# Modulations taken one at a time, a convolution's weights ahead of the first head's decay strips, and two norm broadcasts earlier in TensorE's order

## The chip, the core and the metric

The kernel runs on one core of a Trainium2 chip. The metric is the device time of one execution in microseconds (us), lower is better. A core has five engines that run at the same time, each through its own list of instructions in order: TensorE (PE, matmuls), VectorE (DVE), ScalarE (ACT), GpSimd (POOL) and SyncE (SP). Here SP and POOL mostly issue transfers (DMAs) from memory. An instruction at the head of its engine's list waits on semaphores for the work of other engines, and everything behind it on that engine waits with it.

## The reference

One layer of a diffusion backbone for 512 latent and 256 context tokens of 1024 channels. `c` is the conditioning vector; from it nine modulation vectors (shift, scale and gate, three times) come by one large product.

```python
mods = jnp.split((jax.nn.silu(c) @ w_mod[layer] + b_mod[layer])[:, None, :], N_MOD, axis=-1)
sh1, sc1, g1, sh2, sc2, g2, sh3, sc3, g3 = mods          # the context has its own, from c_ctx
h  = h + 0.5 * g1 * swiglu(modulate(h, norm_ffn1, sh1, sc1), w_ffn1_in, w_ffn1_out)
hc = hc + 0.5 * g1c * swiglu(modulate(hc, norm_ffn1, sh1c, sc1c), w_ffn1_in, w_ffn1_out)
u, uc = modulate(h, norm_mix, sh2, sc2), modulate(hc, norm_mix, sh2c, sc2c)
kv_c = uc @ w_in[:, K0:G0]                               # context keys and values: start states
q, k, v, rg, cv, ga, gb = jnp.split(u @ w_in, IN_SPLITS, axis=-1)
q, k = rope_2d(q, rows, cols), rope_2d(k, rows, cols) * qk_scale
o, _, _ = bidir_retention(q, k, v, log_gf, log_gb, rf, rb)   # 4 heads, decayed scores both ways
h = h + g2 * mixer_output(o, rg, cv, ga, gb, ...)        # gated with a 31-wide depthwise convolution
h = h + 0.5 * g3 * swiglu(modulate(h, norm_ffn2, sh3, sc3), w_ffn2_in, w_ffn2_out)
return rmsnorm(h, final_norm)
```

`modulate(x, w, sh, sc)` is `rmsnorm(x, w) * (1 + sc) + sh`.

## The kernel before

Tokens lie along the free dimension, channels along the 128 partitions. Each product is written as three matmuls (`mm3`, lines 111 to 113): weights and activations are split into a rounded high part and a low rest, and high x high, high x low and low x high are summed. So every weight tile of 128x1024 costs a transfer into one of four `wraw` buffers, a rounding copy on ACT (`wh`, line 102) and a subtraction on DVE (`wl`, line 104).

The order of instructions on each engine isn't the order in which they are written. A scheduler takes the written order as a priority and puts each instruction where its own cost estimates say that its inputs are ready. An edit that moves a call in the text therefore moves instructions only where the scheduler's result changes.

The layer's stages on the time line of the profiled execution, in us from the span's start:

- Up to about 105: the first norm, the first eight modulations (`start`, `first_mods`) and the first products.
- To about 590: the first SwiGLU (`ffn1`). Its hidden blocks come in six groups (`GROUPS1`, of 4, 4, 4, 3, 3 and 4 blocks). A block of the later groups is a `chunk`, seven products of 12 matmuls of 384 columns (`product`, line 404). Behind each group stands the output part: for `mm` in 0 to 3 a weight tile and the products of its two output blocks, added into memory by POOL (`part_sum`). The hidden blocks `hx` are split on ACT and DVE (`split`, lines 300 and 301) just before the output part needs them.
- The other 56 modulation pieces are spread over `ffn1`. `mod_step(count)` takes the next `count` of `MOD_STEPS`; each (`mods`) issues a 512 KB transfer on POOL's queue into one of two `wm` buffers (line 200), and DVE multiplies and sums it (line 206, once or twice). `STEPS_IN` and `STEPS_OUT` say how many fall in each group's chunks and in its output part; several are taken in one call.
- 590 to 650: the second norm and the first head. `tail1` and `head2` hang pieces of the norm between the products. The norm's factor is made per half of the tokens, 256 columns each (first half "a", second half "b"): `rstd_sum` sums squares with four small matmuls (lines 255 and 256), takes a square root on ACT (line 280) and a few small operations on DVE (lines 281 to 286), and makes a diagonal `dg` (line 262). `rstd_bcast` then spreads it over the partitions by one matmul with `ones` (line 269). `norm_mods` makes the normed halves `uh` and `ul` from it: line 291 on DVE, 292 on ACT, 293 on DVE, for each of eight channel blocks.
- In `retention(0)` the context's keys (`keys_c`, 48 matmuls of 256 columns) come first, then `rotated`: keys and queries, for each half of the tokens four products of 24 matmuls. DVE then rotates them (`roped`, lines 733 to 736, and the split in 301). `strips(0)` loads four tables of distances (lines 751 and 752), puts them through Exp on ACT (753, 754) and adds them on DVE (755); scores are multiplied by these strips later. `conv_chunk` (called by `conv_at`) makes one of eight convolution blocks: 48 matmuls of 512 columns and a long chain on DVE (line 716).
- 650 to 1200 the rest of the four heads, to 1380 gates and merging, then the second SwiGLU to the end.

Exp and Sqrt use different tables of ACT: a change from one to the other puts an `ACT_TABLE_LOAD` in its list.

## Time and profile before

| | |
|---|---|
| median of 3 runs | 1781.86 us (1779.5 to 1781.98) |
| the profiled execution's own time | 1779.1 us |
| its span, first to last instruction | 1777.0 us |
| mean granted TensorE clock | 0.985 |
| PE busy / idle in the span | 1723.9 us (97%) / 53.1 us |
| DVE, ACT, POOL busy | 1150.4, 676.0, 141.6 us |
| DMA | 221.97 MB, mean 125 GB/s |

The page and the views of the trace name each instruction by its line in the kernel, its engine, its operation and the tiles that it writes and reads. "Idle before, and what ended it" tells how long an engine sat still before an instruction and whose work released it. PEclk is the clock that TensorE was granted, 1.00 being full speed. Since PE is busy for 97% of the span, the time can fall only where PE waits or where its clock is lowered.

### The profile page before, as it was taken

The numbers are of one execution on the slowest core, as the hardware profiler recorded it, in microseconds if no ns is written. First come the engines' busy times: TensorE is split into PE (matmuls) and PEld (weight loads), VectorE is DVE, ScalarE is ACT, GpSimd is POOL, SyncE is SP. The second block draws the span as 40 slices with busy tenths as digits, with TensorE's granted clock in tenths as the row PEclk, the third lists the DMA queues.
The fourth block names the chain that finished last, engine by engine and source line by source line (L and its number), as shares of the span: only waits on it lengthen the run. The fifth ranks groups of instructions, "written<-read, shape, count | busy, mean of one in ns | idle before, by whom it ended". The sixth has DMA issues, their size and how long they took to land.

```text
span 1777.0 us, 22523 instructions
## 1 busy us (share of the span) xinstructions
PE 1723.9 (97%) x8930; PEld 1498.8 (84%) x8930; DVE 1150.4 (65%) x1818; ACT 676.0 (38%) x969; POOL 141.6 (8%) x221
## 2 busy tenths in 40 slices
PE   5999999999999889999999999999999999999997
PEld 3689999989899878888888888888788988888887
DVE  5895868786677788793885679293765643333335
ACT  4644434434344522342342334233563432222222
POOL 3401020202112100010000000001100000000000
PEclk7999999999999999999999999999999999999999
DMA  9347373857665321142142115115552133222221
GB/s 347 110 143 154 120 182 109 196 177 195 201 171 177 109 83 60 69 157 72 52 156 87 55 69 176 60 48 177 191 196 100 60 119 95 100 95 99 98 84 48
DMA packets 68254, 221.97 MB, mean 125 GB/s; under 512 B 8178, under 2 KB 9202, under 8 KB 68148
## 3 DMA queue, kind: packets, MB, share of 16 engines
q1 hardware_dynamic: 45652, 146.84, 24.6%
q0 software_dynamic: 21920, 72.64, 14.6%
q8 instruction: 70, 1.15, 0.3%
q10 hardware_dynamic: 576, 1.05, 0.2%
q14 instruction: 36, 0.29, 0.0%
HBM read 192.18 MB, written 31.46 MB: 126 GB/s over the span
## 4 chain that ended last, share of the span: by engine, by line
PE 80%; issue 6%; DMA 6%; DVE 6%; ACT 1%; POOL 1%; SPq 0%; DVEq 0%; POOLq 0%; ACTq 0%
PE ps L112 23%; PE ps L113 23%; PE ps L111 23%; PE ps L404 9%; DMA wm<-in_w_mod 2%; DMA th<-in_w_mod 2%; DVE wl L104 1%; DVE h L716 1%; DMA wraw<-in_w_co 1%; DMA wraw<-in_w_v 0%; DMA kl<-in_dec 0%; POOL hdram L620 0%; DVE t L206 0%; DVE t L183 0%; PE ps L895 0%
## 5 line engine op out<-in xcount | busy, mean ns | idle before, releaser
L102 ACT CAST wh<-wraw 128x1024 fp32r<-128x1024 f32 (+2 forms) x212 | 219.5, 1037 | 559.9 <-PE ps L112 309.2
L104 DVE TENSOR_TENSOR wl<-wraw,wh 128x1024 fp32r<-128x1024 f32 (+2 forms) x212 | 254.4, 1203 | 198.3 <-ACT wh L102 193.5
L111 PE MATMUL ps<-uh,wh 128*128 128x512 f32 (+1 forms) x924 | 332.3, 362 | 1.5 <-ACT uh L292 1.1
L113 PE MATMUL ps<-uh,wl 128*128 128x512 f32 (+1 forms) x924 | 331.0, 359 | 0.0
L112 PE MATMUL ps<-ul,wh 128*128 128x512 f32 (+1 forms) x832 | 298.5, 360 | 0.2
L112 PE MATMUL ps<-gx,wh 128*128 128x512 f32 (+1 forms) x544 | 204.0, 377 | 0.0
L113 PE MATMUL ps<-gx,wl 128*128 128x512 f32 (+1 forms) x544 | 204.0, 377 | 0.0
L111 PE MATMUL ps<-gx,wh 128*128 128x512 f32 (+1 forms) x544 | 203.7, 377 | 0.2 <-ACT gx L300 0.2
L111 PEld LDWEIGHTS ps<-uh,wh 128*128 128x128 f32 x924 | 174.8, 190 | 28.2 <-ACT uh L292 1.5
L113 PEld LDWEIGHTS ps<-uh,wl 128*128 128x128 f32 x924 | 175.7, 190 | 25.4 <-issue 0.2
L716 DVE SCALAR_TENSOR_TENSOR h<-y,vec,h 128x512 f32<-128x512 f32 x240 | 179.7, 749 | 5.5
L112 PEld LDWEIGHTS ps<-ul,wh 128*128 128x128 f32 x832 | 158.4, 191 | 24.4 <-issue 0.9
L111 PE MATMUL ps<-hx,wh 128*128 128x512 f32 (+1 forms) x368 | 122.0, 335 | 7.4 <-ACT hx L300 7.4
L112 PE MATMUL ps<-hx,wh 128*128 128x512 f32 (+1 forms) x368 | 123.1, 335 | 0.0
L113 PE MATMUL ps<-hx,wl 128*128 128x512 f32 (+1 forms) x368 | 122.7, 334 | 0.0
L111 PEld LDWEIGHTS ps<-gx,wh 128*128 128x128 f32 x544 | 102.1, 188 | 19.2 <-ACT gx L300 0.4
L112 PEld LDWEIGHTS ps<-gx,wh 128*128 128x128 f32 x544 | 102.0, 188 | 18.7
L113 PEld LDWEIGHTS ps<-gx,wl 128*128 128x128 f32 x544 | 102.0, 188 | 18.7
L359 DVE TENSOR_TENSOR wl<-wraw,wh 128x1024 fp32r<-128x1024 f32 x54 | 66.1, 1224 | 54.5 <-ACT wh L358 54.2
L404 PE MATMUL ps<-th,wl 128*128 128x384 f32 x288 | 96.2, 334 | 0.0
L404 PE MATMUL ps<-th,wh 128*128 128x384 f32 x288 | 96.2, 334 | 0.0
L404 PE MATMUL ps<-tl,wh 128*128 128x384 f32 x288 | 96.2, 334 | 0.0
(277 smaller groups left out, 3109.4 us busy)
## 6 DMA issues: line engine op xcount, KB each, us to landing
wm<-in_w_mod POOLq DMA_DIRECT2D x56, 512.0 KB, 4.5
wraw<-in_w1i SPq DMA_DIRECT2D x44, 512.0 KB, 6.5
wraw<-in_w2i SPq DMA_DIRECT2D x44, 512.0 KB, 3.6
hdram<-sg POOLq DMA_DIRECT2D x40, 384.0 KB, 7.5
wraw<-in_w1o SPq DMA_DIRECT2D x16, 512.0 KB, 3.5
wraw<-in_w_cv SPq DMA_DIRECT2D x16, 512.0 KB, 4.3
wraw<-in_w_v SPq DMA_DIRECT2D x16, 512.0 KB, 6.0
wraw<-in_w_rg SPq DMA_DIRECT2D x16, 512.0 KB, 3.6
```

The lines of the kernel that those rows point to most:

```text
L102: nc.scalar.copy(hi, raw)
L104: nc.vector.tensor_sub(lo, raw, f32(hi))
L111: nc.tensor.matmul(o, w[0], x[0], start=first, stop=False)
L112: nc.tensor.matmul(o, w[0], x[1], start=False, stop=False)
L113: nc.tensor.matmul(o, w[1], x[0], start=False, stop=last)
L359: nc.vector.tensor_sub(lo, src, f32(hi))
L404: nc.tensor.matmul(o, w[i][:, ws], x[k][m], start=first and k == n == 0, stop=k == 3 and n == 2, skip_group_check=True)
L716: nc.vector.scalar_tensor_tensor(o, y[:, t:t + L], vec[:, w0 + t:w0 + t + 1], o, ALU.mult, ALU.add)
```

## The change

Three edits. First, `mod_step` is no longer called with several pieces at a time at the end of a chunk or ahead of an output tile: `spread` deals `STEPS_IN` out over two places in each chunk (one between its products, one behind it, none behind the group's last) and `STEPS_OUT` over the eight output blocks. Second, in the first head `conv_at(0)` is called ahead of `strips(0)`. Third, the first half's broadcast moves from the end of `ffn1` into the context keys: `head2(0)` is called within the first product of `keys_c` and makes the broadcast and all eight blocks; and the second half's broadcast (`head2(2)`) is called behind the first of the four products of `rotated`, not behind the fourth.

```diff
-    def chunk(j, u, t, keep):
+    def chunk(j, u, t, beside, keep):
...
         nc.scalar.activation(s[:, lo_], pa, AF.Silu)
+        beside()
         product(pd, w1, 1, [x[3] for x in t], False)
...
+            steps = spread(STEPS_IN[gi], 2 * nk - 1)
+            beside = lambda: mod_step(next(steps))
             for j in range(2 if k0 == 0 else 0, nk):
...
                 elif k0:
-                    keep(j, chunk(k0 + j, u, t, None))
+                    keep(j, chunk(k0 + j, u, t, beside, None))
+                    beside()
                 if k0:
-                    mod_step(STEPS_IN[gi] * (j + 1) // nk - STEPS_IN[gi] * j // nk)
                     continue
...
+            steps = spread(STEPS_OUT[gi], 8)
             for mm in () if last else range(4):
-                mod_step(STEPS_OUT[gi] * (mm + 1) // 4 - STEPS_OUT[gi] * mm // 4)
...
                 for i in range(2):
+                    beside()
                     part_sum(2 * mm + i, px[i], pc[i][:, :LC])
...
+    def spread(total, slots):
+        return (total * (i + 1) // slots - total * i // slots for i in range(slots))
...
         if n == 4:
             st["a"] = rstd_sum(acc, st["sq", 0], HALVES[0])
-        if n == 6:
-            st["ra"] = rstd_bcast(st["a"])
-        if n == 7:
-            norm_mods(h, st["ra"], deriv["x2"], st["u"], HALVES[0], range(4))
...
         if n == 0:
+            ra = rstd_bcast(st["a"])
+            norm_mods(h, ra, deriv["x2"], u, HALVES[0], range(4))
             st["b"] = rstd_sum(acc, st["sq", 256], HALVES[1])
-            norm_mods(h, st["ra"], deriv["x2"], u, HALVES[0], range(4, KT))
+            norm_mods(h, ra, deriv["x2"], u, HALVES[0], range(4, KT))
...
-                proj(pc[:, i, :], wk[i], uc)
-                if hd == 0:
-                    head2(i)
+                for ks in (range(4), range(4, KT)):
+                    proj(pc[:, i, :], wk[i], uc, ks)
+                    if hd == i == ks[0] == 0:
+                        head2(0)
...
                     proj(px[i][:, c], w[i], u, c=c)
-                if hook:
-                    hook()
-                    hook = None
+                    if hook:
+                        hook()
+                        hook = None
...
+            conv_at(hd)
             sx, sc = strips(hd)
-            conv_at(hd)
```

What becomes of this in the engines' lists, at three places.

DVE at the end of the fourth group (390 us in the profile), where the last hidden block is split and four modulations stand between its steps. Line 206 is a modulation, 421 to 433 the last block's arithmetic, 301 its split. First the kernel before:

```order
L206 SCALAR_TENSOR_TENSOR t_3632,mx<-wm_3630,kh_84 128x1024
L419 TENSOR_TENSOR t_3461<-t_3461,ps_3458 128x384
L230 TENSOR_TENSOR g_x_3634<-mx,vec 128x8
L104 TENSOR_TENSOR wl_3702<-wraw_3698,wh_3700 128x768
L421 TENSOR_TENSOR sg_3464<-ps_3460,t_3461 128x384
```

and the changed one at the same place (its line 420 is 419 of before, 422 is 421):

```order
L206 SCALAR_TENSOR_TENSOR t_3678,mx<-wm_3676,kh_84 128x1024
L420 TENSOR_TENSOR t_3461<-t_3461,ps_3458 128x384
L230 TENSOR_TENSOR g_x_3680<-mx,vec 128x8
L104 TENSOR_TENSOR wl_3698<-wraw_3694,wh_3696 128x768
L422 TENSOR_TENSOR sg_3464<-ps_3460,t_3461 128x384
```

Nothing moved: only the buffers' numbers differ. From the fourth group on, the lists of DVE, ACT and POOL and the waits in them are the same in both kernels up to about 575 us. The first edit changes DVE's list around the first group's output part (some 40 rows), a few neighbours around the second and the third group's, and on POOL's queue the place of one `wm` transfer, which now stands behind two `hdram` sums and not ahead of them.

ACT at the start of the second norm (585 us in the profile). The first Sqrt (line 280) belongs to half "a", the casts (102) to the query weights, lines 292 to the normed blocks. Before:

```order
L102 CAST wh_5661<-wraw_5659 128x1024
L753 ACTIVATE sc_5938<-wraw_5946,lg 128x640
L245 ACTIVATE t_5447<-gx_926_5048 128x256
L280 ACT_TABLE_LOAD
L280 ACTIVATE t_5457<-ps_5451,epsb 128x2
L102 CAST wh_5667<-wraw_5665 128x1024
L754 ACT_TABLE_LOAD
L754 ACTIVATE wraw_5947<-wraw_5947,lg 128x640
```

Now, from that Sqrt to the second one, which belongs to half "b" (lines 758 and 759 are 753 and 754 of before, 783 is 777):

```order
L280 ACTIVATE t_5457<-ps_5451,epsb 128x2
L102 CAST wh_5667<-wraw_5665 128x1024
L245 ACTIVATE t_5480<-gx_927_5049 128x256
L245 ACTIVATE t_5497<-gx_928_5050 128x256
L292 ACTIVATE uh_970_5279<-t_5573,ab_x_3140 128x256
L292 ACTIVATE uh_972_5281<-t_5577,ab_x_3140 128x256
L758 ACT_TABLE_LOAD
L758 ACTIVATE sx_6037<-wraw_6039,lg 128x896
L292 ACTIVATE uh_974_5283<-t_5581,ab_x_3140 128x256
L292 ACTIVATE uh_976_5285<-t_5585,ab_x_3140 128x256
L280 ACT_TABLE_LOAD
L280 ACTIVATE t_5595<-ps_5589,epsb 128x2
```

The strips' Exps left the neighbourhood of half "a"'s Sqrt, which needs no table load any more. The first of them now stands between the normed blocks, ahead of half "b"'s Sqrt. On SP's queue the two transfers of the convolution's weights moved ahead of the strips' four.

PE around the two broadcasts (line 269). Before, the first stands behind the last product of `ffn1` (`hx`), and the second behind all 96 matmuls of the first half:

```order
L113 MATMUL ps_5358<-hx_897_4895,wl_5090 128x256
L269 MATMUL ps_5501<-t_5464,ones 128x256
L111 MATMUL ps_5576<-uh_970_5279,wh_5566 128x256
...
L113 MATMUL ps_5674<-uh_984_5293,wl_5669 128x256
L269 MATMUL ps_5771<-t_5614,ones 128x256
L111 MATMUL ps_5671<-uh_970_5279,wh_5566 128x256
```

Now the first has 27 of the 48 matmuls of the context's keys (`ps_5558`) ahead of it, and the second 12 of the first half's 96 (`ps_5671`):

```order
L113 MATMUL ps_5558<-uh_970_5279,wl_5556 128x256
L269 MATMUL ps_5571<-t_5464,ones 128x256
L111 MATMUL ps_5558<-uh_972_5281,wh_5554 128x256
...
L113 MATMUL ps_5671<-uh_976_5285,wl_5550 128x256
L269 MATMUL ps_5699<-t_5602,ones 128x256
L111 MATMUL ps_5672<-uh_970_5279,wh_5554 128x256
```

Between the two broadcasts PE has 9 matmuls of the context's keys, half "b"'s four small sums, 12 more of the keys and the 12 of the first half. Further on, the 48 matmuls of the convolution block now stand whole ahead of the first scores; before, 4 of them stood ahead and 44 behind the first 11 of the 36 scores' matmuls. DVE makes the low part of the convolution's second weight tile (line 104) behind most of the four rotations, as before.

## The prediction, made before the changed kernel ran

> **What bounds the kernel now.** I read the list of waits of PE first, since PE is busy for 97% of the span (the table above), then each wait in PE's timeline, then the granted clock in short windows, and last DVE and ACT ahead of each wait.

> ```profile
> PE ps L269 <- DVE t L262: 8.7, 3, 5.4
> PE ps L111 <- ACT hx L300: 7.4, 2, 3.8
> PE ps L111 <- ACT gx L300: 4.7, 2, 4.5
> PE ps L111 <- ACT uh L292: 1.1, 1, 1.1
> 594.68 0.79 PE L269 MATMUL ps<-t,ones 128*128 128x256 f32 x1 [5.43 <-DVE t L262]
> 616.91 0.74 PE L111 MATMUL ps<-uh,wh 128*128 128x256 f32 x4 [1.12 <-ACT uh L292]
> 634.26 0.80 PE L111 MATMUL ps<-gx,kh 128*128 128x256 f32 x2 [4.49 <-ACT gx L300]
> ```

> The reader is to see three waits within 45 us, 11.04 us together, all in the stretch that the second and third edit rewrite; and two of 7.4 us in `ffn1`, which the first edit names. Most of the rest of PE's 53 us idle lies at the start and the end of the kernel.

> A wait costs more than its length, since the clock falls. Windows behind the waits at 594.68 and 634.26 (columns: PE, PEld, DVE, ACT, POOL, PEclk, DMA):

> ```profile
> 595.00:597.00 2.00, 2.00 (x9) 1.82 (x9) 1.78 (x5) 0.55 (x2) 0.00 (x0) 0.50 0.90 277
> 597.00:599.00 2.00, 2.00 (x12) 2.00 (x12) 1.78 (x5) 0.94 (x3) 0.00 (x0) 0.56 0.77 301
> 634.00:636.00 2.00, 1.68 (x5) 1.17 (x6) 1.96 (x4) 0.21 (x1) 0.00 (x0) 0.50 0.00 0
> 636.00:638.00 2.00, 2.00 (x9) 1.99 (x10) 2.00 (x4) 0.63 (x1) 0.00 (x0) 0.50 0.00 0
> 638.00:640.00 2.00, 2.00 (x6) 1.51 (x5) 2.00 (x3) 0.00 (x0) 0.00 (x0) 0.57 0.64 217
> ```

> Time lost is busy time x (1 - clock). From 594.68: 0.32 x 0.5 + 2 x 0.5 + 2 x 0.44 = 2.0. From 634.26: 1.74 x 0.5 + 2 x 0.5 + 2 x 0.43 = 2.7. So the stretch loses 11.0 + 4.7 = 15.7 us.

> **Edit one, the modulations: 0 us.** The waits for `hx` come from a modulation whose transfer is late, with the last block's arithmetic queued behind it on DVE:

> ```profile
> 386.15 0.53 POOL L200 DMA_DIRECT2D wm<-in_w_mod  x1 [3.51 <-DMA wm<-in_w_mod]
> 390.26 1.23 DVE L206 SCALAR_TENSOR_TENSOR t<-wm,kh 128x1024 bf16<-128x1024 f32 x1 [3.93 <-DMA wm<-in_w_mod]
> 397.45 1.65 PE L111 MATMUL ps<-hx,wh 128*128 128x512 f32 x4 [3.82 <-ACT hx L300]
> 120.00:140.00 20.00, 20.00 (x128) 18.07 (x127) 19.66 (x40) 6.95 (x10) 5.02 (x8) 1.00 0.70 216
> ```

> The lists of DVE, ACT and POOL there, and at the second of these waits, are the same before and after, so the same transfer is late for the same instruction. What did move lies at 120 to 160 us, where PE has no idle time to lose. There DVE is nearly full, so an `hx` split could come late. Bounds: a gain of both waits and of clock as behind the 594.68 one, 7.4 + 2 x 2.0 = 11.4 us, or a new wait like the 3.8 seen here. I take 0, the equal lists.

> **Edits two and three, the first broadcast: its 5.43 us wait and 2.0 us of clock go.** Work on DVE and ACT ahead of it now:

> ```profile
> 588.39 1.28 ACT L280 ACT_TABLE_LOAD   x1
> 589.69 0.26 ACT L280 ACTIVATE t<-ps,epsb 128x2 f32<-128x2 f32 x1
> 588.97 0.28 PE L113 MATMUL ps<-hx,wl 128*128 128x256 f32 x1
> 590.96 1.07 DVE L755 TENSOR_TENSOR sx<-sx,wraw 128x896 f32<-128x896 f32 x1
> 592.21 1.22 DVE L104 TENSOR_TENSOR wl<-wraw,wh 128x1024 fp32r<-128x1024 f32 x1
> 593.41 0.82 DVE L755 TENSOR_TENSOR sc<-sc,wraw 128x640 f32<-128x640 f32 x1
> 594.14 0.48 DVE L262 TENSOR_SCALAR t<-ident_h,t 128x128 f32<-128x128 f32 x2
> 599.91 0.28 PE L255 MATMUL ps<-ones,acc 128*128 128x2 f32 x2
> 600.73 0.36 PE L111 MATMUL ps<-uh,wh 128*128 128x256 f32 x1
> 615.20 0.59 PE L269 MATMUL ps<-t,ones 128*128 128x256 f32 x2
> ```

> A matmul of 256 columns takes (615.20 - 600.73) / 120 = 0.12 us. PE now has 27 of them behind its last `hx` matmul, so it comes to the broadcast at 588.97 + 28 x 0.12 = 592.3. DVE needs no strips (1.07 + 0.82) and no table load (1.28) first; from the Sqrt, about 588.3 (the four sums stand some 11 matmuls earlier and no load follows), it has two `wl` (2.4), a residual (0.48) and the small chain (1.1): 592.3 too. I take no wait; the bounds are 0 and the 1.22 of one `wl` late.

> **The second broadcast brings a new wait of 3.6 us.** It has moved forward by 84 matmuls, and ACT isn't ready for it. The order on ACT and DVE, walked with these rows:

> ```profile
> 596.45 1.31 ACT L292 ACTIVATE uh<-t,ab_x 128x256 fp32r<-128x256 f32 x3 [2.48 <-DVE t L291]
> 579.43 1.05 ACT L753 ACTIVATE sx<-wraw,lg 128x896 f32<-128x896 f32 x1
> wraw<-in_dist_x SPq DMA_DIRECT2D x8, 448.0 KB, 3.7
> wraw<-in_w_v SPq DMA_DIRECT2D x16, 512.0 KB, 6.0
> 601.20 0.16 DVE L281 TENSOR_SCALAR t<-ps 128x2 f32<-128x2 f32 x1 [1.35 <-ACT t L280]
> 602.05 0.49 DVE L262 TENSOR_SCALAR t<-ident_h,t 128x128 f32<-128x128 f32 x2
> 606.50 0.68 DVE L778 SCALAR_TENSOR_TENSOR gc<-ps,gc 128x512 fp32r<-128x512 f32 x1
> ```

> Broadcast "a" ends at 592.8. ACT does two normed blocks (to 594.5, paced by DVE), a table load for Exp (595.8), the strip's Exp (596.8; its transfer waits for the last-but-one `wl`, about 591.3, and lands 3.7 later, so in time), two more blocks (597.7), a table load for Sqrt (599.0) and the Sqrt (599.2). DVE's chain takes 602.54 - 601.20 = 1.3, with line 778 (0.68) now within it: 601.2. PE comes there after 9 + 12 keys, four small sums (600.73 - 599.91 = 0.8, rows above) and 12 matmuls: 592.8 + 33 x 0.12 + 0.8 = 597.6. The wait is 601.2 - 597.6 = 3.6 us, in pieces: about 0.8 for blocks 2 and 3, then 2.8 at the broadcast itself. Bounds: 1.3 if the load and the Exp (2.3) hide, and 3.6 + 2.3 = 5.9 if the distances take the 6.0 of `in_w_v` and not 3.7. I take 3.6, by the transfer's own row. In exchange the 1.12 at 616.91 goes: half "b" is made from a broadcast at 601.2 and not at 615.20.

> Does that new wait of 2.8 lower the clock? The nearest rows are a wait of 2.45 at the start and one of 1.54 later:

> ```profile
> 38.11 0.22 PE L180 MATMUL ps<-ident,t 2*128 2x2 f32 x1 [2.45 <-DVE t L179]
> 38.00:40.00 2.00, 1.89 (x8) 1.30 (x9) 2.00 (x7) 2.00 (x5) 0.08 (x1) 0.74 1.05 398
> 40.00:42.00 2.00, 2.00 (x7) 0.98 (x6) 2.00 (x5) 0.46 (x2) 2.00 (x2) 0.50 1.04 385
> 1277.55 0.70 PE L269 MATMUL ps<-t,ones 128*128 128x512 f32 x1 [1.54 <-DVE t L262]
> 1278.00:1280.00 2.00, 2.00 (x9) 1.43 (x8) 1.34 (x3) 1.99 (x4) 0.53 (x1) 1.00 0.02 8
> ```

> 2.45 did, for 1.89 x 0.26 + 2 x 0.5 = 1.5 us; 1.54 did not. 2.8 is nearest to the first: 1.5, between 0 and the 2.7 found above.

> [...]

> **The convolution ahead of the scores: the 4.49 us wait and 2.7 us of clock go, 0.6 us come.** PE waited for the rotated queries; now 48 matmuls of the convolution (twice the columns: about 0.24 each, 11.5 us) stand ahead. What is late next is the low part of the second weight tile, on DVE behind most of the rotations:

> ```profile
> 623.37 0.69 DVE L733 TENSOR_TENSOR t<-ps,rope 128x512 f32<-128x512 f32 x1 [0.87 <-PE ps L113]
> ```

> PE leaves the broadcast at 601.7, has 84 + 96 matmuls (21.6) and the 1.5 of clock: 624.8. The first 24 of the convolution don't need that tile: 630.6. The first keys are whole after 108 of the 180, at 616.2; from there DVE has 18 operations of 0.7 and two `wl`, 15.0 us, to 631.2. The wait is about 0.6; bounds 0 and the 4.5 that it replaces. The queries are whole a rotation's sum, a `wl` and a split later (2.6), at 633.8; PE wants them after 24 more matmuls, at 637.0, and doesn't wait.

> **Sum.** Gone: 11.0 + 4.7 = 15.7. New: 3.6 + 1.5 + 0.6 = 5.7. The change gains 10.0 us. The profiled execution took 1779.1 (span 1777.0 and 2.1 around it): 1769.1 by that. The median of the runs stands 2.8 higher: 1771.9 by that. I forecast 1771, between the two.

> **Rivals.** (1) The modulations gain too: both `hx` waits go, 10.0 + 11.4 = 21.4 us, 1760. For it speaks only what the calls say; against it the equal lists. 4%. (2) The new waits take nearly all: 5.9 at the broadcast, 2.7 of clock, 4.5 at the convolution, a gain of 2.6, 1778. Each end is possible, all three at once are not likely; a slower ACT start by 2 us does two of them. 10%. (3) Slower: ACT stands in order, so the strip's Exp holds up blocks 2 and 3, the second Sqrt and PE for every microsecond that the distances land after 595. Slower by 0.2% (3.6 us) needs 10.0 + 3.6 = 13.6 us more, about 17 us from issue to landing. The slowest median among the transfers of up to 512 KB is that of the first loads:

> ```profile
> hx<-in_xT SPq DMA_DIRECT2D x8, 256.0 KB, 9.5
> ```

> 4%, with an unseen wait of another cause in it. (4) The clock holds through the 2.8 us: 11.5, 1769.5; this lies within the forecast.

> **Numbers.** The forecast's own cases reach from a gain of 4 to one of 14.5 (15.7 less the low end 1.3): 80%; 2% lie between that and rival 1. Range: 1765 (1779.1 - 14.5) to 1777.5 (1781.9 - 4). Faster by over 0.2%, which is about what a measurement of this kernel can tell from no change: 0.86. Within it: 0.10. Slower: 0.04.

> **What would show it.** In the changed profile: the two `hx` waits near 397 and 471 still there; no wait above 1 us at the first line 269; one of about 2.8 us at the second, with PEclk at 0.50 in the next 4 us; a short wait for `wl` in the convolution and none for `gx`; the rest of the kernel the same, shifted. Wrong would be: the `hx` waits gone, a wait of over 6 us at the second broadcast, or a DVE that, once PE runs ahead of it, makes PE wait in the heads from 650 on.

## Result and profile after: 9.5 us faster

The changed kernel takes 1770.0 us (median of 5 runs, 1766.58 to 1773.25), the kernel before 1779.5 in the same comparison (5 runs). The ratio is 0.9949, 95% interval [0.9927, 0.9971], 9 us. A second comparison gave 0.9951 [0.9933, 0.9969]. The profiled execution is the slowest of the first five, 1773.25, with a span of 1771.4.

From PE's list of waits, changed kernel (us in total, times, longest):

```profile
PE ps L111 <- ACT hx L300: 7.0, 2, 3.7
PE ps L269 <- DVE t L262: 6.8, 3, 2.7
PE ps L111 <- ACT uh L292: 0.5, 1, 0.5
```

The line for `gx` has sunk to 0.2 us and the one for `uh` is 0.5 for 1.1; the two waits for `hx` are as they were. Line 269 still stands at 6.8 us: the first broadcast's 5.43 is gone from it, the second broadcast's is new, and the one at the layer norm near 1270 us is longer. PE's timeline in the second norm and the first head, and at the end of that stage, where the values begin (before: 588.97 and 651.64):

```profile
589.33 0.28 PE L113 MATMUL ps<-hx,wl 128*128 128x256 f32 x1
592.68 0.65 PE L269 MATMUL ps<-t,ones 128*128 128x256 f32 x2
598.02 0.38 PE L111 MATMUL ps<-uh,wh 128*128 128x256 f32 x1 [0.48 <-ACT uh L292]
601.83 0.70 PE L269 MATMUL ps<-t,ones 128*128 128x256 f32 x2 [2.39 <-DVE t L262]
631.85 0.50 PE L113 MATMUL ps<-uh,wl 128*128 128x512 f32 x1 [0.68 <-DVE wl L104]
641.78 0.40 PE L111 MATMUL ps<-wh,uh 128*128 128x512 f32 x1
```

The first broadcast has no wait, the second has one of 2.39 with 0.48 ahead of it, the convolution one of 0.68. From the last `ffn1` matmul to the values the stage takes 641.78 - 589.33 = 52.5 us; before it took 651.64 - 588.97 = 62.7. That is 10.2 us of gain in this one stage.

The span is only 5.6 us shorter. The rest was given back at one place, the layer norm's broadcast (line 269 again). The row for the kernel before is in the prediction (1277.55, a wait of 1.54). Now, with the clock behind it (columns: PE, PEld, DVE, ACT, POOL, PEclk, DMA):

```profile
1269.34 2.08 PE L269 MATMUL ps<-t,ones 128*128 128x512 f32 x2 [2.74 <-DVE t L262]
1265.70 1.23 DVE L979 TENSOR_TENSOR wraw<-wraw,wraw 128x1024 f32<-128x1024 f32 x1 [3.28 <-DMA wraw<-ypart]
1260.00:1270.00 10.00, 7.26 (x31) 5.62 (x30) 6.58 (x16) 6.01 (x7) 0.53 (x1) 0.93 0.51 175
1270.00:1272.00 2.00, 2.00 (x4) 1.00 (x3) 1.18 (x3) 1.24 (x2) 1.06 (x2) 0.50 0.07 20
1272.00:1274.00 2.00, 2.00 (x6) 1.54 (x5) 2.00 (x3) 0.56 (x2) 0.00 (x0) 0.50 0.95 283
1274.00:1276.00 2.00, 2.00 (x7) 1.55 (x7) 1.46 (x3) 1.99 (x3) 0.00 (x0) 0.64 1.03 379
```

Ahead of the small operations that make the diagonal, DVE's list holds a sum of the heads' parts (line 979) that waits for its transfer. PE came there some 9.4 us earlier than before, but the transfer let DVE go on only 8.2 us earlier (1273.90 before, 1265.70 now). So the wait grew by 1.2 us, and this time it lowered the clock. It fell during the wait, so only the 0.66 us from 1269.34 to 1270 were computed at 0.50 in the first window: 0.66 x 0.5 + 2 x 0.5 + 2 x 0.5 + 2 x 0.36 = 3.1 us. Together 4.3, which closes the account: 10.2 - 0.4 (lost up to 589) - 4.3 = 5.5, against 5.6 of span.

### The profile page after: what moved, and what is told of

The parts are those of the page before. It is cut to its first block, busy times and chain, and to the rows that moved or that the text cites. A ratio compares the mean times of both kernels' runs of the same rounds, so it can differ in the third digit from the quotient of the medians.

```text
span 1771.4 us, 22518 instructions
## 1 busy us (share of the span) xinstructions
PE 1721.9 (97%) x8930; PEld 1498.3 (85%) x8930; DVE 1150.3 (65%) x1818; ACT 675.1 (38%) x968; POOL 141.8 (8%) x221
## 3 DMA queue, kind: packets, MB, share of 16 engines
q10 hardware_dynamic: 576, 1.05, 0.2%
## 5 line engine op out<-in xcount | busy, mean ns | idle before, releaser
L104 DVE TENSOR_TENSOR wl<-wraw,wh 128x1024 fp32r<-128x1024 f32 (+2 forms) x212 | 254.6, 1203 | 192.1 <-ACT wh L102 187.5
L111 PE MATMUL ps<-uh,wh 128*128 128x512 f32 (+1 forms) x924 | 334.8, 363 | 0.8 <-ACT uh L292 0.5
L113 PE MATMUL ps<-uh,wl 128*128 128x512 f32 (+1 forms) x924 | 332.0, 360 | 1.5 <-DVE wl L104 1.5
L113 PE MATMUL ps<-gx,wl 128*128 128x512 f32 (+1 forms) x544 | 204.1, 377 | 0.0
L111 PE MATMUL ps<-gx,wh 128*128 128x512 f32 (+1 forms) x544 | 203.8, 378 | 0.2 <-ACT gx L300 0.2
L111 PEld LDWEIGHTS ps<-uh,wh 128*128 128x128 f32 x924 | 175.7, 191 | 28.1 <-issue 0.7
L113 PEld LDWEIGHTS ps<-uh,wl 128*128 128x128 f32 x924 | 175.7, 190 | 27.8 <-DVE wl L104 2.4
L111 PE MATMUL ps<-hx,wh 128*128 128x512 f32 (+1 forms) x368 | 121.7, 334 | 7.0 <-ACT hx L300 7.0
L113 PE MATMUL ps<-hx,wl 128*128 128x512 f32 (+1 forms) x368 | 123.2, 335 | 0.0
L111 PEld LDWEIGHTS ps<-gx,wh 128*128 128x128 f32 x544 | 102.1, 188 | 19.1 <-ACT gx L300 0.4
L113 PEld LDWEIGHTS ps<-gx,wl 128*128 128x128 f32 x544 | 102.0, 188 | 18.6
L359 DVE TENSOR_TENSOR wl<-wraw,wh 128x1024 fp32r<-128x1024 f32 x54 | 66.1, 1224 | 52.6 <-ACT wh L358 52.5
## 6 DMA issues: line engine op xcount, KB each, us to landing
wm<-in_w_mod POOLq DMA_DIRECT2D x56, 512.0 KB, 4.6
wraw<-in_w1i SPq DMA_DIRECT2D x44, 512.0 KB, 6.2
wraw<-in_w2i SPq DMA_DIRECT2D x44, 512.0 KB, 3.8
wraw<-in_w1o SPq DMA_DIRECT2D x16, 512.0 KB, 3.6
wraw<-in_w_cv SPq DMA_DIRECT2D x16, 512.0 KB, 3.8
wraw<-in_w_v SPq DMA_DIRECT2D x16, 512.0 KB, 5.7
wraw<-in_w_rg SPq DMA_DIRECT2D x16, 512.0 KB, 3.7
```

Source lines behind the costliest of these rows:

```text
L104: nc.vector.tensor_sub(lo, raw, f32(hi))
L111: nc.tensor.matmul(o, w[0], x[0], start=first, stop=False)
L113: nc.tensor.matmul(o, w[1], x[0], start=False, stop=last)
L359: nc.vector.tensor_sub(lo, src, f32(hi))
```

## Experiments

All ratios are to the kernel before, timed on the same chip beside it. "us" is that ratio's distance from 1 times the median of before. The first four rows, the next four, the next three and the last come from four chips, so between these groups the ratios compare better than the medians.

| kernel | median us | ratio [95%] | us |
|---|---|---|---|
| edit one alone | 1780.37 | 0.9996 [0.9983, 1.0008] | -0.7 |
| edit two alone | 1777.69 | 0.9979 [0.9966, 0.9992] | -3.7 |
| edit three alone | 1769.45 | 0.9934 [0.9922, 0.9947] | -11.8 |
| edits two and three | 1768.57 | 0.9930 [0.9918, 0.9942] | -12.5 |
| whole change again | 1770.79 | 0.9951 [0.9933, 0.9969] | -8.7 |
| whole, second broadcast later | 1767.44 | 0.9935 [0.9919, 0.9951] | -11.6 |
| whole, strips held | 1767.03 | 0.9936 [0.9919, 0.9953] | -11.4 |
| whole, modulations held | 1789.83 | 1.0064 [1.0045, 1.0083] | +11.4 |
| whole, modulations dealt evenly | 1762.48 | 0.9898 [0.9881, 0.9915] | -18.2 |
| whole, one 4-byte tile more | 1779.74 | 1.0001 [0.9991, 1.0011] | +0.2 |
| strips held and modulations even | 1758.30 | 0.9876 [0.9858, 0.9895] | -22.1 |
| the same, layer norm's broadcast later | 1766.97 | 0.9926 [0.9909, 0.9944] | -13.2 |

### The three edits apart

Edit one alone is the first hunk of the diff (`spread` and `beside`) and nothing else.

> The kernel before with edit one alone (modulations dealt one at a time). Theory: 0 us, within 0.2% of before, since the two waits for hx near 397 and 471 us (7.4 us before, 7.0 after the whole change) stay, as do the first broadcast's 5.4 and the wait for gx of 4.5; the only trace of the edit is two waits of 0.5 us on hx in the early groups, 1 us slower at most. Rival: dealing the modulations out is part of the gain: 3 us or more faster.

It measures as no change. PE's waits are those of before, and two small ones on `hx` in the early groups (0.9 us together). PE's list and timeline of this kernel:

```profile
PE ps L111 <- ACT hx L300: 6.2, 2, 3.3
595.13 1.22 PE L269 MATMUL ps<-t,ones 128*128 128x256 f32 x2 [5.54 <-DVE t L262]
634.60 0.80 PE L111 MATMUL ps<-gx,kh 128*128 128x256 f32 x2 [4.48 <-ACT gx L300]
```

Edit two alone:

```diff
+            conv_at(hd)
             sx, sc = strips(hd)
-            conv_at(hd)
```

> The kernel before with edit two alone (the convolution ahead of the strips). Theory: two gains. The wait for gx (4.49 and 2.7 of clock) becomes one of about 0.7 for a weight's low part: 6.5 us. And the strips leave ACT's and DVE's lists ahead of the first Sqrt, with a table load (1.28): half a's diagonal is ready at about 592.5 and not 594.6, so the first broadcast's wait goes from 5.4 to about 3.2: 2.2 us. Together 8 to 9 us faster. Rival: the broadcasts' places carry that part, and this edit gives only the 6.5 us at the convolution, or less if the strips' Exps now make half b late.

Only the smaller half of the expectation came: 3.7 us. The wait at the first broadcast fell to 3.02, as expected, but the wait for `gx` is still there, whole:

```profile
593.08 0.78 PE L269 MATMUL ps<-t,ones 128*128 128x256 f32 x2 [3.02 <-DVE t L262]
632.35 0.79 PE L111 MATMUL ps<-gx,kh 128*128 128x256 f32 x2 [4.49 <-ACT gx L300]
```

In PE's list of this kernel only 4 of the convolution's 48 matmuls stand ahead of the first scores, as before. Calling the convolution ahead of the strips did not move it ahead of the scores.

Edit three alone is the hunks of `tail1`, `head2`, `keys_c` and `rotated`.

> The kernel before with edit three alone (the two broadcasts moved in TensorE's order). Theory: the wait for gx stays (4.5 and 2.7 of clock). The first broadcast still has the strips and a table load ahead of it on ACT and DVE, so its diagonal stays at 594.6; PE comes 27 matmuls later (3.1 us): a wait of about 2.4 and 1.5 of clock for 5.4 and 2.0. At the second one ACT has no strip in the way: 0 to 0.5. The 1.1 of half b goes. About 4 us faster. Rival: the broadcasts' places are the change: 8 us or more faster.

The rival is right: 11.8 us. In this kernel PE has all 48 of the convolution's matmuls ahead of the scores, and all 48 of the keys' (not 27) ahead of the first broadcast. Its timeline:

```profile
592.19 0.62 PE L269 MATMUL ps<-t,ones 128*128 128x256 f32 x2
593.72 0.38 PE L255 MATMUL ps<-ones,acc 128*128 128x2 f32 x2 [0.91 <-DVE acc L246]
598.78 1.22 PE L269 MATMUL ps<-t,ones 128*128 128x256 f32 x2
628.63 0.50 PE L113 MATMUL ps<-uh,wl 128*128 128x512 f32 x1 [0.69 <-DVE wl L104]
```

So it is the earlier broadcasts that change the place of the convolution. The scheduler decides that by its own estimate of when the rotated keys and queries are ready; why it comes out so was not tried.

The changed kernel without the first hunk (`spread`, `beside`):

> The changed kernel without edit one, so edits two and three together. Theory: as the whole change, 9 to 11 us faster than before (ratio 0.994 to 0.995), perhaps by 1 us more, since the two waits of 0.5 us on hx in the early groups are not there. Edits two and three overlap at the first broadcast, so together they give less than the sum of the two alone (8.5 + 4). Rival: the whole change needs edit one: less than 7 us faster.

Edits two and three together give 12.5 us, no more than edit three alone within the intervals. The stage from the last `ffn1` matmul to the values takes 62.6 us with edit one, 60.0 with edit two, 52.2 with edit three, 51.3 with two and three and 52.5 with all. Edit three carries the change. Whether edit one takes some 3.5 us back (12.5 without it, 9 and 8.7 with it) isn't settled, since the intervals overlap and edit one alone measures as no change.

### The second broadcast's wait

The changed kernel as it is, with nothing edited:

> The changed kernel once more, beside the kernels of this call. Theory 1 (edit one costs nothing): 11 to 12.5 us faster than before, as edits two and three without it (12.3). Theory 2 (edit one costs 2 to 3 us by its two small waits in the early groups): 9 to 10 us faster. At the second broadcast a wait of 2.4 us again, and in its profile the clock behind it either falls to 0.50 (1.7 us) or stays, if what decides is how the wait lies in the clock's own time and not its length.

The wait of 2.4 us is there again (2.38 at 605.93), and the clock falls behind it. In the kernel without edit one the same wait of 2.39 left the clock alone. First that one's rows, then those of the repeated run:

```profile
603.55 0.70 PE L269 MATMUL ps<-t,ones 128*128 128x256 f32 x2 [2.39 <-DVE t L262]
604.00:606.00 2.00, 1.71 (x14) 1.48 (x13) 1.59 (x5) 2.00 (x4) 0.00 (x0) 1.00 0.00 0
606.00:608.00 2.00, 2.00 (x19) 2.00 (x19) 2.00 (x6) 1.77 (x5) 0.00 (x0) 1.00 0.02 4
```

```profile
605.93 0.70 PE L269 MATMUL ps<-t,ones 128*128 128x256 f32 x2 [2.38 <-DVE t L262]
606.00:608.00 2.00, 2.00 (x11) 1.80 (x12) 1.75 (x5) 1.99 (x5) 0.00 (x0) 0.78 0.00 0
608.00:610.00 2.00, 2.00 (x10) 2.00 (x11) 2.00 (x6) 1.77 (x5) 0.00 (x0) 0.50 0.02 4
610.00:612.00 2.00, 2.00 (x17) 2.00 (x16) 2.00 (x6) 1.12 (x3) 0.00 (x0) 0.87 0.56 168
```

Then two ways to be rid of it. The broadcast one product later:

```diff
-                    if hook:
+                    if hook and i == 1:
```

> The changed kernel with the second broadcast one product later (behind the first two of the four products). Theory (PE gets there before the diagonal, which ACT's list delays to 601.8 us whatever PE does): 12 more matmuls, 1.5 us, stand ahead of it, its wait falls from 2.4 to about 0.9, too short to lower the clock: 1.5 to 3.2 us faster than the changed kernel, 1766 to 1768.5. Rival: half b's blocks come later by as much and PE waits for them at the next 96 matmuls: no gain.

Its median lies 3.4 us below that of the whole change beside it, as the theory says, but the intervals of the two ratios overlap. In the profiles the stage from the last `ffn1` matmul to the values is 2.6 us shorter (49.8 for 52.4). The wait fell only to 1.85, not to 0.9, and with the wait for `uh` ahead of it that makes 0.9 of the 2.6; the other 1.7 are the clock's loss, which isn't there (2 us at 1.00 where the repeated run had 0.50):

```profile
603.14 0.70 PE L269 MATMUL ps<-t,ones 128*128 128x256 f32 x2 [1.85 <-DVE t L262]
604.00:606.00 2.00, 1.92 (x16) 1.71 (x15) 1.80 (x5) 2.00 (x6) 0.00 (x0) 1.00 0.04 8
```

The strips held back by their data:

```diff
+        if hd == 0:
+            held = cp.tile([P, 2], F32, name="held")
+            for i, g in enumerate((gf, gb)):
+                nc.vector.scalar_tensor_tensor(held[:, i:i + 1], f32(u[7][1][:, L - 1:L]), 0.0, g, ALU.mult, ALU.add)
+            gf, gb = held[:, 0:1], held[:, 1:2]
```

> The changed kernel with the strips' Exps held behind half b's last normed block (their scale is made to depend on it). Theory (the 2.4 us at the second broadcast are ACT's: a load of Exp's table 1.28, an Exp 1.05 and the load of Sqrt's table back 1.28 stand ahead of half b's Sqrt): all three leave, the diagonal is ready 2.3 to 3.6 us earlier, the waits there (0.5 + 2.4) fall below 0.5, no clock is lost: 2.4 to 4.1 us faster than the changed kernel, 1766 to 1767.5. Rival: DVE's blocks of half a are what is late, and the wait stays above 1.5; or the scores then wait for the strips.

Both table loads and the Exp have left ACT's list between the halves, and the wait fell from 2.39 to 1.48, not below 0.5: PE is still there before half b's chain is done. The median is 3.8 us below the whole change's, again with overlapping intervals; in its profile the stage itself is only 1.2 us shorter (51.2 for 52.4), and more was gained ahead of it, at the two waits for `hx`, which this edit doesn't touch. The clock fell even behind 1.48 us:

```profile
598.41 0.98 PE L269 MATMUL ps<-t,ones 128*128 128x256 f32 x2 [1.48 <-DVE t L262]
599.00:601.00 2.00, 2.00 (x10) 1.91 (x10) 2.00 (x6) 1.08 (x3) 0.00 (x0) 0.50 0.59 213
601.00:603.00 2.00, 2.00 (x15) 2.00 (x15) 2.00 (x7) 1.31 (x3) 0.00 (x0) 0.72 0.05 12
```

### The modulations and the waits for hx

In the changed kernel DVE's list holds five modulations (line 206) between the split of the fourth group's second hidden block (379.57) and that of its last. Two of them have their data; the others come at the pace of the transfers. The timeline of the changed kernel, with DVE's last step for that block (line 434) and ACT's cast that PE waits for (line 300):

```profile
385.56 1.22 DVE L206 SCALAR_TENSOR_TENSOR t<-wm,kh 128x1024 bf16<-128x1024 f32 x1
390.77 1.22 DVE L206 SCALAR_TENSOR_TENSOR t<-wm,kh 128x1024 bf16<-128x1024 f32 x1 [3.51 <-DMA wm<-in_w_mod]
395.19 1.22 DVE L206 SCALAR_TENSOR_TENSOR t<-wm,kh 128x1024 bf16<-128x1024 f32 x1
396.81 0.56 DVE L434 TENSOR_TENSOR sg<-sg,sg 128x384 f32<-128x384 f32 x1
397.40 0.51 ACT L300 CAST hx<-sg 128x384 fp32r<-128x384 f32 x1 [1.56 <-DVE sg L434]
```

PE wants the block at 394.6 (its matmul starts at 397.96 after a wait of 3.32). The block's last step stands behind all of them, and the three shown came one each 4.4 to 5.2 us. To keep them away the scalar 1.0 of the output part's modulations is made from the last split, so that no scheduler can put them ahead of it; the chunks take four, the output part eight:

```diff
-                junk, raw, 1.0, ccrow[v], ALU.mult, ALU.mult, accum_out=dst[:, j:j + 1])
+                junk, raw, one[0], ccrow[v], ALU.mult, ALU.mult, accum_out=dst[:, j:j + 1])
...
+            if gi in (3, 4):
+                one[0] = t_((P, 1), F32, "one")
+                nc.vector.tensor_scalar(one[0], f32(g[-1][1][:, LA - 1:LA]), 0.0, 1.0, ALU.mult, ALU.add)
```

> The changed kernel with the modulations of the fourth and fifth group kept out of the last chunk: four dealt over the first two chunks, eight over the output part, and these eight held behind the last hx split (their scalar 1.0 is made from it). Theory (the two hx waits come from modulations that stand in DVE's list between the last chunk's steps, and their late transfers): both waits go, 3.3 and 3.7 us, with the clock behind them (1.7 and 1.6): 7 to 10 us faster than the changed kernel, 1760 to 1763. Rival: the transfers are late all the same and DVE stands before the next group's chunks: the waits move there, gain below 3 us.

19 us slower than the whole change beside it, in two parts. The rival is one: the waits for `hx` are gone, but ten modulations now stand ahead of the next group's first chunk, and PE waits there 5.62 and 6.1 us (line 406 is 404 of the changed kernel):

```profile
PE ps L406 <- DVE t L420: 11.7, 2, 6.1
430.69 1.23 DVE L208 SCALAR_TENSOR_TENSOR t<-wm,kh 128x1024 bf16<-128x1024 f32 x1 [1.79 <-DMA wm<-in_w_mod]
436.17 0.69 PE L406 MATMUL ps<-uh,wh 128*128 128x384 f32 x1 [5.62 <-DVE t L420]
```

The other part was expected by neither: from 1280 us on this kernel fell back by another 10.7 us against the repeated run, with no new wait. 1.6 of them are clock behind the layer norm's wait; for the rest PE waited no longer than there. In the second SwiGLU it does fewer matmuls in the same time at the same granted clock. The changed kernel first, then this one:

```profile
1500.00:1600.00 100.00, 100.00 (x443) 82.83 (x442) 34.05 (x36) 25.66 (x31) 0.00 (x0) 1.00 0.30 95
```

```profile
1500.00:1600.00 100.00, 100.00 (x431) 80.66 (x430) 34.03 (x37) 24.19 (x28) 0.00 (x0) 1.00 0.29 93
```

Of what the edit adds, the tile `one` of 4 bytes per partition was the suspect. Both parts were tried at once. With the scalar in a column of a tile that exists, and the modulations dealt so that DVE finds at most three between the last two splits and eight at most ahead of the next chunk:

```diff
+            steps = iter({3: [1, 1, 1, 2, 1], 4: [1, 1, 1, 2, 1]}[gi]) if gi in (3, 4) else spread(STEPS_IN[gi], 2 * nk - 1)
...
+            steps = iter({3: [0, 1, 1, 1, 1, 1, 1, 0], 4: [0, 1, 1, 1, 1, 1, 1, 0]}[gi]) if gi in (3, 4) else spread(STEPS_OUT[gi], 8)
...
+                one[0] = dots[:, 0, 0, 0:1]
```

> The changed kernel with the modulations of the fourth and fifth group dealt six over the chunks, of which DVE has at most three between the last two hidden splits, and six over the output part, held behind the last hx split; the held scalar lies in a tile that is there already. Theory (DVE can take one modulation about every 4 us, two of them at once; five between the last two splits were too many, and ten between a group's end and its next chunk as well): no wait at hx and none at the next chunk, 7.0 to 7.9 of waits and about 3 of clock gone: 7 to 10 us faster than the changed kernel, 1760 to 1763, and the second SwiGLU runs at 443 matmuls per 100 us again. Rival: the transfers are what is short, the waits move on to another chunk: gain below 3 us.

The theory holds: 9 us faster than the whole change by the ratios (18.2 against 9 and 8.7), 8 by the medians. No wait for `hx` is left, the chunks wait 2.2 us in all, and the second SwiGLU runs at its old pace:

```profile
PE ps L406 <- DVE t L420: 2.2, 2, 1.2
1500.00:1600.00 100.00, 100.00 (x443) 82.81 (x442) 33.57 (x36) 26.02 (x32) 0.00 (x0) 1.00 0.31 94
```

And the tile by itself:

```diff
+            if gi in (3, 4):
+                nc.vector.memset(t_((P, 1), F32, "one"), 1.0)
```

> The changed kernel with nothing but a tile of one 4-byte column more per partition (written twice, never read), in the pool that holds the weight buffers. Theory (the run with held modulations lost 10.7 us behind 1280 us because the new 4-byte tile moves the buffers behind it to other addresses): 431 matmuls per 100 us at 1500 to 1700 us, not 443, and 10 us slower than the changed kernel, 1780. Rival (that loss comes from the changed order): 443 per 100 us, 1769 to 1772.

The theory holds here too: 1779.74, which is 9 to 10 us more than the changed kernel against the same kernel before, with the slow pace:

```profile
1500.00:1600.00 100.00, 100.00 (x432) 80.53 (x431) 34.02 (x36) 25.09 (x30) 0.00 (x0) 1.00 0.29 91
```

PE's list is the same as the changed kernel's at all 8930 places, so nothing but their pace differs. That a tile of 4 bytes slows the matmuls is shown. That it does so through the addresses of the tiles behind it is the author's guess and not shown: the trace has no addresses.

### Together

The held strips and the evenly dealt modulations in one kernel, the diffs of both:

> The changed kernel with the strips held behind half b's last block and with the modulations dealt as in the run beside it. Theory: the two gains lie in different stages and add up: 3 to 4 and 7 to 10 us faster than the changed kernel, 1757 to 1761, ratio 0.987 to 0.990. Rival: what is gained early is given back where transfers set the pace, at the layer norm near 1270 us (its wait 2 to 3 us and above with the clock behind it): 1762 or more.

The two gains add up, within the intervals: 1758.3 us, ratio 0.9876, the fastest kernel of this study, 12 us below the changed one. The rival is there as well, in part: the layer norm's wait has grown to 3.50 us. The second broadcast waits 1.48 us as in the run with the strips alone held, and here the clock stays at 1.00 behind it:

```profile
592.41 0.70 PE L271 MATMUL ps<-t,ones 128*128 128x256 f32 x2 [1.48 <-DVE t L264]
1259.42 1.92 PE L271 MATMUL ps<-t,ones 128*128 128x512 f32 x2 [3.50 <-DVE t L264]
593.00:595.00 2.00, 2.00 (x19) 2.00 (x18) 2.00 (x6) 1.09 (x3) 0.00 (x0) 1.00 0.60 206
```

The last run tried to take it away by a later broadcast:

```diff
-        if m == 4:
+        if m == 5:
             st["rl"] = rstd_bcast(st["dg"])
-        for j in range(2 * (m - 4), 2 * (m - 3)) if m >= 4 else ():
+        for j in range(0 if m == 5 else 2 * (m - 4), 2 * (m - 3)) if m >= 5 else ():
```

> Both fixes, and the layer norm's broadcast near 1260 us one gate block later (48 matmuls of 512 columns, 11 us), with its first four blocks made together. Theory: the wait there (3.5 us in the profile of both fixes, 1.5 to 3.1 in the other kernels, and 0 to 2.5 of clock behind it) ends, since the diagonal, held up on DVE by a transfer of the heads' sums, is 11 us early: 2 to 5 us faster than both fixes, 1753 to 1756.5. Rival: the last normed blocks come too late for the merging products, a wait of 2 us or more at about 1290 us takes the place: 1757 to 1760.

By the ratios it is 8.9 us slower than both fixes, so the rival is right that another wait takes the place, but not in its cause, and the time lies above both ranges. The broadcast at 1269.03 no longer waits. The blocks' Silus, pushed back, now alternate in ACT's list with the gates' Sigmoids, and seven table loads (9.0 us) fall between 1280.5 and 1297.1; behind them stands the cast of the next weights, and PE waits longer than before:

```profile
1298.24 0.80 PE L111 MATMUL ps<-gx,wh 128*128 128x512 f32 x1 [6.39 <-ACT wh L102]
```

With 2.7 us of clock behind it this wait costs 9.1 us; the one that it replaces cost 5.1 (3.50 and 1.6). That is 4.0 of the 6.4 us by which the two spans differ. The clock at the second broadcast, lowered in this profile and not in the other, is 1.5 more, and 1.1 lies ahead of the first broadcast.

## Why the prediction was right, step by step

- **Edit one, 0 us.** Right: alone it measures -0.7 us, and the `hx` waits stay. The bound of 11.4 us for both waits and their clock was of the right size too: dealing the modulations at the transfers' pace brought 8 to 9.
- **First broadcast, 5.43 and 2.0 of clock gone.** Right: predicted at 592.3 with no wait, measured 592.68 with none.
- **Second broadcast, a new wait of 3.6.** Right in kind, 0.7 too large: 0.48 + 2.39 = 2.87. The broadcast was forecast for 601.2 and came at 601.83, and PE came a little later than worked out. Its cause, ACT's table load and Exp, is shown by the run with the strips held, but only for 0.9 of the 2.39: PE would still be early by 1.48.
- **The clock behind it, 1.5 us.** The size was right in this profile, by luck: 3.41 x 0.5 = 1.7, by the second row below. The step's reasoning, that a wait's length decides by the nearest row, failed: 2.39 cost nothing in one run and 1.48 cost 1.6 us in another (2 x 0.5 + 2 x 0.28, from 599 to 603). What separated the two in these traces is told below.

```profile
599.61:603.02 3.41, 1.19 (x8) 1.14 (x9) 2.98 (x12) 3.06 (x6) 0.00 (x0) 1.00 0.37 146
603.02:606.43 3.41, 3.41 (x17) 3.32 (x17) 3.23 (x9) 3.18 (x8) 0.00 (x0) 0.50 0.05 10
```

- **The convolution: 4.49 and 2.7 of clock gone, 0.6 new.** Right: 0.68, for the weight's low part, as named. What the prediction left together and the expectation then put to edit two is edit three's doing.
- **The sum, 10.0.** The stage gained 10.2. "The rest of the kernel the same, shifted" is the step that failed: the layer norm near 1270 us is paced by a transfer, came 8.2 us earlier where PE came 9.4 earlier, and gave back 4.3 us in the profiled execution. That execution gained 5.6 us of span, the medians 9.5: that the number came so near to 10.0 is in part luck. Where the broadcast stands as in the change, its wait is 1.45 to 3.50 us (0.46 and 0.99 in two kernels), and its clock fell in some only. That, with the start (the longest wait there is 10.4 to 13.3 us in these profiles), may be why single runs of one kernel lie 6 us apart; only one execution of each was profiled.
- **The range.** 1781.9 - 4 is 1777.9 and not 1777.5. Nothing hangs on it.

## What to carry to other kernels

Cost a stage by its own waits (that gave 10.0 us for the 10.2 measured here), and then look down the program for the next place that a transfer paces: what is gained ahead of it can end there as a longer wait, as 4.3 us did here with the clock behind it. Where a scheduler sets the order, take the edits apart before saying which one moved what; here the one that was meant for the convolution didn't move it, and another did. A modulation, or any work that hangs on transfers, belongs in an engine's list at the transfers' pace (8 to 9 us here), and a false data dependence is a way to keep a scheduler from putting it earlier.

## What the runs showed of the hardware

**The clock's price was not set by the length of one wait here.** Waits of 1.85 and 2.39 us (above) left the clock at 1.00, and so did one of 2.84 at the layer norm, below, in the kernel with edit three alone; waits of 2.38, 2.39 and 2.74 lowered it to 0.50. One of 1.48 lowered it with the strips held and did not with both fixes, where the same instructions stand there. Two stretches of the kernel with edit three alone, with the 2.84 in their middle:

```profile
1265.46 1.12 PE L269 MATMUL ps<-t,ones 128*128 128x512 f32 x2 [2.84 <-DVE t L262]
1260.63:1264.04 3.41, 1.99 (x9) 1.31 (x7) 2.22 (x7) 0.17 (x1) 0.00 (x0) 1.00 0.53 214
1264.04:1267.45 3.41, 1.99 (x7) 1.34 (x8) 3.02 (x9) 3.38 (x4) 0.53 (x1) 1.00 0.43 154
```

The 2.84 above is cut in half by the mark at 1264.04, so PE is busy for 1.99 us on each side. The 2.39 of the changed kernel lies with 2.22 in one stretch, where PE is busy for 1.19 (above). Of the three kernels with 1.48, the two in which the clock fell (strips held, and the last run) have a shorter wait of 0.34 between the same two marks; with both fixes a mark lies between them. Where the marks fall differs from execution to execution: at 603.02 and at 607.11 in the two profiles of the changed kernel, 4.09 apart. So the kernel alone doesn't tell what a wait of 1.5 to 3.4 us will cost; one of 3.40 near 398 us, in the run with the 4-byte tile, was cut by a mark and cost no clock.

**A tile of 4 bytes per partition cost 9 to 10 us.** 431 or 432 matmuls per 100 us for 443, 2.5 to 2.7%, at a granted clock of 1.00 and with no wait. Matched place by place with the changed kernel, PE's list falls back by 8.1 us from 1400 us on, by 1.3 between 1300 and 1350 and by 2.1 in the heads, between 800 and 1260; shorter waits in this profile hide part of it. So a third way to lose time stands beside the two named ahead of the prediction, PE's waits and its clock. Here the scalar in a column of a tile that is there cost nothing of the kind.
